# A decoder layer on one TensorE: q and k by Strassen's seven products, in a stage of their own ahead of the convolution's projections

## The chip, the cores and the metric

The kernel runs on one NeuronCore of a Trainium2 chip. The metric is the device time of one execution in microseconds. The kernel before takes 2086.06 us, the median of three runs (2084.89 to 2089.5).

## The reference

One decoder layer over 512 tokens of width 2048, all in float32. The combined input projection has columns q, k, v (1024 each: attention) and B, C, h (1024 each: a gated short convolution).

```
hn = rms_norm(x, norm_mix_pre)
q, k, v, gate_b, gate_c, hc = split(hn @ w_in)
a = diff_attention(q, k, v, lam, rel_bias)       # 8 heads of 128, two softmaxes of 64 each, causal
a = rms_norm(a, subln_gain) * (1 - lambda_init)
c = rms_norm(gate_b * short_conv(gate_c * hc, conv_w), conv_norm_gain)
x = x + rms_norm(concat(a, c) @ w_out, norm_mix_post)
hn = rms_norm(x, norm_ffn_pre)
f = (silu(hn @ w_gate) * (hn @ w_up)) @ w_down   # 5632 wide
x = x + rms_norm(f, norm_ffn_post)
```

The attention subtracts lam times a second softmax from the first; each head's scores get a bias by distance.

## The kernel before, in words

**Operands.** Every float32 operand of a product is held as two parts, high and low (`split`, L97 to L100: ScalarE casts the high part, VectorE subtracts it from the source for the low part). `mm3` (L121 to L130) makes one product of three matmuls: high by high (L124), high by low (L125), low by high (L126). Each matmul has its own weight load of 128 x 128.

**Places.** The transposed activations lie in `acts` as `act_hi` and `act_lo` (16 floats from the tile's start) and later, for the feed-forward part, as `ffn_hi` and `ffn_lo` (0 floats from the start). Behind `acts` in the same pool lie four ring slots of 2048 floats (`ring_tile`, L85), each a tile of its own. A weight chunk takes two slots (high, low); a Strassen operand of 128 columns takes one. A ring slot is written again when the products that read it are through. A pool that opens where another closed puts its tiles over the old ones, so a first write waits for the last read of the old tile.

**The order of the work.** A list of jobs (`add_job`, L157) is run in order by `run_jobs`. A job names the weight chunks that it needs; `run_jobs` loads them one chunk ahead (`load_chunk`: a 1 MB load on the queue of SyncE, then a split into two ring slots). A job is a generator: each time it yields, `side_step` lets every generator in the list `side` make one step. So what lies in `side` is placed between pieces of a job's matmuls. The tile framework places the instructions of each engine in an order of its own near the program's.

**Stages.** First the norm, the transposes of x and the first half of v's columns; then v's second half (`job_v`, 4 chunks of 4 yields, 12 matmuls of 512 columns each). Then, for each of four pairs of heads, `job_cols` (L342) for q, k, h, c and b: two halves of the contraction, each with two pieces of 24 matmuls (128 weights' columns by 512 tokens). `done_q` and `done_k` (L371 to L395) split q and k from PSUM. Behind k of a pair, the generator `heads` for its two heads goes into `side`: 12 steps beside the 12 pieces of h, c and b. A step does `scores` of one query tile, `values` of the tile two steps before, `weights` (the transposes of the softmax weights, L458) of the tile one step before, and sometimes `head_out`. v stays in SBUF (`v_sb`), as do `aT`, `cT` and the other tiles of the attention pool `attn`, opened right after the first stage. Then come the output projection (`job_out`), the feed-forward part by Strassen products (`ffn`: gate and up as 44 quartets of seven products with 24 matmuls of 256 columns; then down, 12 blocks of seven products in two halves) and the tail.

In gate and up, `prepare` makes the weights' operand of each product four products ahead: a sum or difference of two quarters of the weights (`combine`), then a split into one ring slot. `gather` adds the finished products. The moving operands are `acts` for four of the seven products and tiles named x for the sums of activations in the other three.

Of the kernel before, what the change touches and what calls it, by code (L numbers as in the profile page):

```python
# [18 lines left out]
P = 128  # L19
# [36 lines left out]
def trunk(ctx: ExitStack, tc: tile.TileContext, a, out):  # L56
# [45 lines left out]
    def rsqrt_mean(ss, n, width, eps, name):  # L102
# [3 lines left out]
        nc.gpsimd.tensor_tensor(out=r, in0=v, in1=mhalf[:, :n], op=ALU.pow)  # L106
        return r

    def load_chunk(src, n, m, name, parts=None):

        raw = wp.tile([P, n, m], F32, tag="raw", name=f"raw_{name}")
        nc.sync.dma_start(raw, src.rearrange("(n p) m -> p n m", p=P))
        if parts is None:
            hi = ring_tile(n, m, f"hi_{name}")
            lo = ring_tile(n, m, f"lo_{name}")
        else:
            hi, lo = parts(name)
        split(hi, lo, raw)
        return hi, lo

# [36 lines left out]
    def add_job(specs, go, ahead=1):  # L157
        jobs.append((specs, go, ahead))
# [25 lines left out]
    with start as sp:  # L184
# [124 lines left out]
    ap_ = at.enter_context(tc.tile_pool(name="attn", bufs=1))  # L309
    aT = ap_.tile([P, NH, S], F32, name="aT")  # L310
    cT = ap_.tile([P, 8, S], F32, name="cT")
    v_sb = ap_.tile([P, NT, A], F32, name="v_sb")
    sqacc = ap_.tile([P, S], F32, name="sqacc")

    klos = [ap_.tile([P, 2, S], F32R, name=f"klo{i}") for i in range(2)]
    for t in klos:
        nc.gpsimd.memset(t.bitcast(F32), 0.0)

    for t in range(NT):
        nc.scalar.copy(v_sb[:, t, :512], vb[t])  # L320

    def job_v(cg, q4, banks):
        def go(ch):
            (hi, lo), = ch
            for t in range(NT):
                if q4 == 0:
                    banks.append(mm_bank(f"pv_{cg}_{t}"))
                for k in range(4):
                    kc = 4 * q4 + k
                    mm3(banks[t], act_hi[:, t, kc, :], act_lo[:, t, kc, :], hi[:, k, :], lo[:, k, :], kc == 0, kc == KC - 1)  # L330
                if q4 == 3:
                    nc.scalar.copy(v_sb[:, t, cg * 512 : (cg + 1) * 512], banks[t])
                yield

        add_job([v_spec(cg, q4)], go)
# [4 lines left out]
    def job_cols(w, c0, name, done, after=None):  # L340

        banks = []  # L342

        def part(half):
            def go(ch):
                (hi, lo), = ch
                for j in range(2):
                    if half == 0:
                        banks.append(mm_bank(f"pc_{name}_{j}"))
                    for k in range(8):  # L350
                        kc = 8 * half + k
                        cs = slice(j * P, (j + 1) * P)
# [4 lines left out]
                if half == 1 and after is not None:  # L357
                    side.append(after())

            return go  # L360

        for half in range(2):
            add_job([col_spec(w, c0, half, name)], part(half))

    qk = {}

    halves = ((slice(0, QK), slice(QK, P)), (slice(QK, P), slice(0, QK)))  # L370

    def done_q(hp):
        def done(j, b):
            h = 2 * hp + j
            q = ap_.tile([P, 2, S], F32R, tag="q", bufs=2, name=f"q_{h}")
            for c, (own, other) in enumerate(halves):
                nc.scalar.copy(q[own, c, :], b[own, :])
                nc.vector.tensor_sub(q[other, c, :], b[own, :], q[own, c, :].bitcast(F32))
            qk["q", h] = q

        return done

    def done_k(hp):
        def done(j, b):
            h = 2 * hp + j
            k = ap_.tile([P, 2, S], F32R, tag="k", bufs=2, name=f"k_{h}")
            lo = klos[h % 2]
            for c, (own, other) in enumerate(halves):
                nc.scalar.copy(k[own, c, :], b[own, :])
                nc.scalar.copy(k[other, c, :], b[own, :])  # L390
                nc.vector.tensor_sub(lo[own, c, :], b[own, :], k[own, c, :].bitcast(F32))
            qk["k", h] = k, lo

        return done

    def heads(hs):

        at_ = [(h, qt) for h in hs for qt in range(NT)]
        st = {}
        for i in range(len(at_) + 4):  # L400
            if i < len(at_):
                scores(*at_[i], st)
            if 2 <= i <= len(at_) + 1:
                values(*at_[i - 2], st)
            if 1 <= i <= len(at_):
                weights(*at_[i - 1], st)
            if 4 <= i and at_[i - 4][1] == NT - 1:
                head_out(at_[i - 4][0], st)
            yield

    def scores(h, qt, st):
        if qt == 0:
# [10 lines left out]
        q, (k, klo), bt = qk["q", h], qk["k", h], st["bt", h]  # L423
        n = (qt + 1) * P
        qs = slice(qt * P, n)
        pss = [aux_bank(f"pss_{h}_{qt}_{c}") for c in range(2)]
# [347 lines left out]
    raws, heads_raw, operands, psq, tmp, slots, begun, made = {}, {}, {}, {}, {}, {}, {}, {}  # L774

    def slot(kind):

# [71 lines left out]
    def prepare(n):  # L849

        if n >= len(order):
            return prepare_down(n - len(order))
        q, i = order[n]
        if (q, i) in STAGED:

            if n < 2:
                w = wp.tile([P, 16, P], F32R, tag="raw", name=f"w_{q}_{i}")
            elif n == 2:
                w = place("spare", F32R, (P, 16, P))
            else:  # L860
                w = ring_tile(16, P, f"w_{q}_{i}")
            nc.sync.dma_start(w.rearrange("p k m -> p (k m)").bitcast(F32), stg[STAGED.index((q, i))])
            operands[n] = w.rearrange("p (a k) m -> p a k m", a=2)
        else:
            src = source(q, i)
            if i == 7 and q >= HEAD:
                combine(q, 3)
            if i == (3 if q == last_q else 6):
                combine(q, 2)
            if i == 3:  # L870
                combine(q, 4)
            w = ring_tile(16, P, f"w_{q}_{i}").rearrange("p (a k) m -> p a k m", a=2)
# [195 lines left out]
    def prepare_down(n):  # L1068
# [15 lines left out]
        w = ring_tile(2 * len(ks), 256, f"w_d{n}").rearrange("p (a k) m -> p a k m", a=2)  # L1084
        made["down"] = split(w[:, 0], w[:, 1], src)
        operands_d[n] = w
        if hf == 1:
# [125 lines left out]
    def tail_loads(i, hf):  # L1213
# [14 lines left out]
        if i == 4:  # L1228
            tail_split(1, tmp["tail", 1])
            for cg in (2, 3):  # L1230
                raw = tail_raw(cg, place(turns[count_b[0] % 3], F32, (P, 4, 512)))
                count_b[0] += 1
                ch[cg] = [ring_tile(4, 512, f"w_t{cg}_{part}") for part in range(2)]
                tail_split(cg, raw)

    def down_last(_):
# [69 lines left out]
```

## Time and profile before

| | |
|---|---|
| median of three runs | 2086.06 us |
| the profiled execution, its own time | 2091.33 us |
| its span, first to last instruction | 2089.5 us |
| TensorE busy | 2066.4 us (99%), 14604 matmuls |
| VectorE busy | 1499.9 us (72%) |
| ScalarE busy | 915.7 us (44%) |
| moved by DMA | 345.87 MB, 166 GB/s on the mean |
| granted TensorE clock | 0.996 |

PE is TensorE's matmuls, PEld its weight loads, DVE VectorE, ACT ScalarE, POOL GpSimd, SP the queue of SyncE that issues most DMAs. Tiles are named as in the program, out <- in. Matmuls are pipelined: a row's duration overlaps the next, so the pace is read from the starts. A `pc_q` is a bank of q's projection, `pv` of v's, `pss` scores, `ptw` transposed softmax weights, `pa` (from `w`, `acts`) and `pb` banks of gate and up, `pd` of down, `po` of the output projection. Where an instruction waited, the row's bracket or last column says how long and for whom.

### The profile page before, as it was taken

Reading aid. Unit: us, or ns where it says so; the run is one execution under the profiler, and the core shown is the slowest. Engines: PE = TensorE matmul, PEld = TensorE weight load, DVE = VectorE, ACT = ScalarE, POOL = GpSimd, SP = SyncE. Lnnn points to the kernel's source line nnn. Section 1 sums busy time; section 2 is a strip of 40 time slices with the busy share of each in tenths; the row PEclk is TensorE's granted clock in tenths of the full one; section 3 lists DMA queues with packets and bytes.
Section 4 is the critical chain, followed back from the end, with each engine's and each line's share of the span. In section 5 each row is a group of like instructions: output and inputs, shape, how many; then the busy total and the mean of one; then the engine's idle time right before and its main releaser. Section 6 shows DMA issues by size and latency. Waiting matters only on the chain.

```text
span 2089.5 us, 34251 instructions
## 1 busy us (share of the span) xinstructions
PE 2066.4 (99%) x14604; PEld 1927.1 (92%) x14604; DVE 1499.9 (72%) x1899; ACT 915.7 (44%) x1269; POOL 29.2 (1%) x51
## 2 busy tenths in 40 slices
PE   8999999999999999999999999999999999999998
PEld 6888888888888889999999999999999999999996
DVE  5226445363565368988888898988888777888887
ACT  4234343342444345444445544554544444444442
POOL 0000000000000000000000000000000000000000
PEclk9999999999999999999999999999999999999999
DMA  7432232223219868545454454454554965848454
GB/s 236 132 101 86 86 106 76 91 91 100 82 61 355 292 234 301 164 150 157 139 169 157 140 170 156 155 164 146 157 170 137 320 197 164 295 118 292 123 187 161
DMA packets 297049, 345.87 MB, mean 166 GB/s; under 512 B 11544, under 2 KB 261400, under 8 KB 291136
## 3 DMA queue, kind: packets, MB, share of 16 engines
q1 hardware_dynamic: 295296, 337.90, 49.5%
q10 hardware_dynamic: 1600, 5.79, 0.8%
q8 instruction: 114, 1.87, 0.4%
q14 instruction: 39, 0.32, 0.0%
HBM read 282.82 MB, written 63.46 MB: 166 GB/s over the span
## 4 chain that ended last, share of the span: by engine, by line
PE 93%; DVE 3%; DMA 2%; ACT 1%; issue 0%; SPq 0%; POOL 0%; POOLq 0%; DVEq 0%; ACTq 0%
PE pb L125 7%; PE pb L124 7%; PE pb L126 7%; PE pd L126 6%; PE pd L125 6%; PE pd L124 6%; PE pa L124 5%; PE pa L125 5%; PE pa L126 5%; PE po L124 3%; PE po L126 3%; PE po L125 3%; PE pv L125 1%; PE pv L126 1%; PE pv L124 1%; PE pc_h L124 1%
## 5 line engine op out<-in xcount | busy, mean ns | idle before, releaser
L125 PE MATMUL pb<-x,w 128*128 128x256 f32 x704 | 197.0, 280 | 0.0
L124 PE MATMUL pb<-x,w 128*128 128x256 f32 x704 | 196.6, 279 | 0.0
L126 PE MATMUL pb<-x,w 128*128 128x256 f32 x704 | 196.5, 279 | 0.0
L125 PE MATMUL pb<-acts,w 128*128 128x256 f32 x704 | 195.3, 277 | 0.0
L124 PE MATMUL pb<-acts,w 128*128 128x256 f32 x704 | 195.3, 277 | 0.0
L126 PE MATMUL pb<-acts,w 128*128 128x256 f32 x704 | 195.3, 277 | 0.0
L124 PE MATMUL pa<-acts,w 128*128 128x256 f32 x696 | 193.7, 278 | 0.0
L125 PE MATMUL pa<-acts,w 128*128 128x256 f32 x696 | 193.2, 278 | 0.0
L126 PE MATMUL pa<-acts,w 128*128 128x256 f32 x696 | 193.0, 277 | 0.0
L98 ACT CAST w<-raw_q 128x1024 fp32r<-128x1024 f32 x124 | 130.2, 1051 | 138.2 <-PE pb L126 66.1
L124 PE MATMUL pd<-w_d,acts 128*128 128x256 f32 x640 | 176.9, 276 | 1.0 <-DMA acts<-hx 1.0
L126 PE MATMUL pd<-w_d,acts 128*128 128x256 f32 x640 | 176.9, 276 | 1.0 <-DMA acts<-hx 1.0
L125 PE MATMUL pd<-w_d,acts 128*128 128x256 f32 x640 | 176.7, 276 | 0.0
L99 DVE TENSOR_TENSOR w<-raw_q,w 128x1024 fp32r<-128x1024 f32 x124 | 150.9, 1219 | 21.0 <-ACT w L98 20.7
L125 PE MATMUL pd<-w_d,x 128*128 128x256 f32 x480 | 132.6, 276 | 0.3 <-DVE w_d L99 0.3
L126 PEld LDWEIGHTS pb<-acts,w 128*128 128x128 f32 x704 | 132.8, 189 | 0.0
L124 PE MATMUL pd<-w_d,x 128*128 128x256 f32 x480 | 132.5, 276 | 0.0
L126 PE MATMUL pd<-w_d,x 128*128 128x256 f32 x480 | 132.5, 276 | 0.0
L124 PEld LDWEIGHTS pb<-x,w 128*128 128x128 f32 x704 | 132.3, 188 | 0.0
L125 PEld LDWEIGHTS pb<-acts,w 128*128 128x128 f32 x704 | 132.2, 188 | 0.0
L124 PEld LDWEIGHTS pb<-acts,w 128*128 128x128 f32 x704 | 132.2, 188 | 0.0
L125 PEld LDWEIGHTS pb<-x,w 128*128 128x128 f32 x704 | 132.1, 188 | 0.0
(304 smaller groups left out, 6074.5 us busy)
## 6 DMA issues: line engine op xcount, KB each, us to landing
raw_q<-in_w_gate SPq DMA_DIRECT2D x42, 1024.0 KB, 5.2
post<-in_w_up SPq DMA_DIRECT2D x22, 1024.0 KB, 5.2
pre<-in_w_up SPq DMA_DIRECT2D x22, 1024.0 KB, 5.4
hx<-spare SPq DMA_DIRECT2D x20, 896.0 KB, 8.5
hx<-m SPq DMA_DIRECT2D x20, 896.0 KB, 9.3
raw_o<-in_w_out SPq DMA_DIRECT2D x16, 1024.0 KB, 8.7
raw_b<-in_w_down SPq DMA_DIRECT2D x16, 896.0 KB, 6.3
acts<-hx SPq DMA_DIRECT2D x32, 448.0 KB, 9.0
```

Of the source, the lines that this page charges most:

```text
L98: first = nc.scalar.copy(hi, src)
L99: second = nc.vector.tensor_tensor(out=lo, in0=src, in1=hi.bitcast(F32), op=ALU.subtract)
L124: yield nc.tensor.matmul(o, lhsT=lhi, rhs=rhi, start=start, stop=False, **kw).ins
L125: yield nc.tensor.matmul(o, lhsT=lhi, rhs=rlo, start=False, stop=False, **kw).ins
L126: yield nc.tensor.matmul(o, lhsT=llo, rhs=rhi, start=False, stop=stop, **kw).ins
```

## The change

q and k are no longer projected between the convolution's columns. Right after v, a job `project` computes them in eight quartets (four pairs of heads, q and k) of Strassen's seven products, as gate and up do: tokens and the contraction are cut in halves, a weights' block of 256 columns in four quarters, and each product is 8 k x 3 matmuls of 256 columns. The four sums of activations (`t_sums`) are made beside v's second half into `t_all`. The tiles of this stage lie in a pool `wino`, opened where the attention pool was opened before and closed when the products are done; only then does the attention pool open. q, k and v are therefore written to DRAM (`qkd`, `vd`) and read again: v as a whole behind h's first job, q and k head by head into a part of `aT` that is not yet in use (`load_qk`, `prepare_head`, which splits them as `done_q` and `done_k` did). All eight heads are one generator of 37 steps, which starts beside c's first job. The raw weights and first operands of h are prepared inside `project`. `lamv` moves from the constants into `wino`. The ring becomes one tile of four slots 2080 floats apart in place of four tiles of 2048; the new stage uses each slot 16 floats further on, all others at its start.

```
-    ring = [0]
+    ring = [1]
+    ring_all = high.tile([P, 4 * (D + 32)], F32R, name="ring_all")
-    def ring_tile(n, m, name):
+    def ring_tile(n, m, shift=0):
         i = ring[0] = (ring[0] + 1) % 4
-        return high.tile([P, n, m], F32R, tag=f"ring{i}", name=name)
+        return ring_all[:, (D + 32) * i + shift :][:, : n * m].rearrange("p (n m) -> p n m", n=n)
...
+    wino = ExitStack()
+    wn = wino.enter_context(tc.tile_pool(name="wino", bufs=1))
+    t_all = wn.tile([P, 8 * D + 16], F32R, name="t_all")
+    odd_raw = [wn.tile([P, D], F32, name=f"odd{i}") for i in range(2)]
-    lamv = const.tile([P, 4, QK], F32, name="lamv")
+    lamv = wn.tile([P, 4, QK], F32, name="lamv")
...
+    def evacuate(cg, t, bank):
+        if t % 2 == 0:
+            tmp["v"] = wn.tile([P, 2, 512], F32, tag="r", bufs=2, name=f"r_v{cg}_{t}")
+        nc.scalar.copy(tmp["v"][:, t % 2, :], bank)
+        if t % 2:
+            nc.sync.dma_start(vd[:, t - 1 : t + 1, cg * 512 : (cg + 1) * 512], tmp["v"])
...
+    def open_attn(_):
+        wino.close()
+        ap_ = at.enter_context(tc.tile_pool(name="attn", bufs=1))
...
+    def load_attn(_):
+        load_qk(0)
+        nc.sync.dma_start(v_sb, vd)
+        side.append(heads(range(NH)))
...
                 if q4 == 3:
-                    nc.scalar.copy(v_sb[:, t, cg * 512 : (cg + 1) * 512], banks[t])
+                    evacuate(cg, t, banks[t])
+                    if t < 2:
+                        load_qk_raw(0, t)
+                    else:
+                        prepare_qk(t - 2)
...
+    def t_sums():
+        for tau in range(2):
+            a_, b_, c_, d_ = (odd_raw[j // 2][:, 1024 * (j % 2) :][:, :1024] for j in range(4))
...
+            whole(a_, 2 + tau, 0)
+            whole(b_, tau, 0)
+            nc.vector.tensor_sub(b_, a_, b_)
+            keep(5, b_)
+            yield
...
+    def prepare_qk(n):
...
+        if i in (7, 6, 3):
+            combine_qk(q, {7: 3, 6: 2, 3: 4}[i])
...
+        w = ring_tile(16, P, 16).rearrange("p (a k) m -> p a k m", a=2)
+        split(w[:, 0], w[:, 1], src)
...
+    def project(_):
+        for half in range(2):
+            load_qk_raw(1, half)
+        ready, st = 2, {}
+        for n, (q, i) in enumerate(order_qk):
...
+            for k in range(8):
+                mm3(o, w[:, 0, k, :], w[:, 1, k, :], xh[:, :, k, :], xl[:, :, k, :], k == 0 and i in (1, 5), k == 7, shared=True)
+            yield
...
+            while ready < n + 4:
+                prepare_qk(ready)
+                ready += 1
...
+    def load_qk(h):
+        if h < NH:
+            nc.sync.dma_start(aT[:, 6:8, :], qkd[:, h])
...
+    def prepare_head(h):
...
+        for c, (own, other) in enumerate(halves):
+            b = aT[own, 6, :]
+            nc.scalar.copy(q[own, c, :], b)
+            nc.vector.tensor_sub(q[other, c, :], b, q[own, c, :].bitcast(F32))
...
+        load_qk(h + 1)
...
     def heads(hs):
+        prepare_head(0)
+        yield
...
+            if i < len(at_) and at_[i][1] == 1 and at_[i][0] < NH - 1:
+                prepare_head(at_[i][0] + 1)
             yield
...
+    side.append(t_sums())
+    add_job([], project, ahead=0)
+    add_job([], open_attn, ahead=0)
     for p in range(4):
-        job_cols(w_in, p * 256, f"q{p}", done_q(p))
-        job_cols(w_in, A + p * 256, f"k{p}", done_k(p), after=lambda p=p: heads((2 * p, 2 * p + 1)))
         job_cols(w_in, 3 * A + 2 * A + p * 256, f"h{p}", done_h)
+        if p == 0:
+            add_job([], load_attn)
         job_cols(w_in, 3 * A + A + p * 256, f"c{p}", done_c(p))
         job_cols(w_in, 3 * A + p * 256, f"b{p}", done_b(p))
```

More of the change, by code (lines that the diff above doesn't have):

```diff
@@ L306, in trunk @@
             nc.sync.dma_start(cw[:, i, :], a["conv_w"][0, i].rearrange("(j p) -> p j", p=P))
-    at = ctx.enter_context(ExitStack())
[L309 to L320, printed above, removed]
+    vd = dram.tile([P, NT, A], F32, name="vd")
+    qkd = dram.tile([P, NH, 2, S], F32, name="qkd")
+    def evacuate(cg, t, bank):
[4 more added lines that the diff above has]
+            nc.sync.dma_start(vd[:, t - 1 : t + 1, cg * 512 : (cg + 1) * 512], tmp["v"])
+    tmp = {}
+    for t in range(NT):
+        evacuate(0, t, vb[t])
+    at = ctx.enter_context(ExitStack())
+    ap_ = aT = cT = v_sb = sqacc = klos = None
+    def open_attn(_):
+        nonlocal ap_, aT, cT, v_sb, sqacc, klos
+        wino.close()
+        ap_ = at.enter_context(tc.tile_pool(name="attn", bufs=1))
+        v_sb = ap_.tile([P, NT, A], F32, name="v_sb")
+        aT = ap_.tile([P, NH, S], F32, name="aT")
+        cT = ap_.tile([P, 8, S], F32, name="cT")
+        sqacc = ap_.tile([P, S], F32, name="sqacc")
+        klos = [ap_.tile([P, 2, S], F32R, name=f"klo{i}") for i in range(2)]
+        for t in klos:
+            nc.gpsimd.memset(t.bitcast(F32), 0.0)
+        return
+        yield
[3 more added lines that the diff above has]
+        side.append(heads(range(NH)))
+        return
+        yield
     def job_v(cg, q4, banks):
@@ L363, in job_cols, with t_part, whole, keep @@
             add_job([col_spec(w, c0, half, name)], part(half))
+    T_PLACE = {5: 0, 7: 1, 6: 2, 4: 3}
+    order_qk = [(q, i) for q in range(8) for i in (1, 5, 7, 2, 6, 3, 4)]
+    raws_qk, operands_qk = {}, {}
+    def t_part(i, part):
+        return t_all[:, 16 + (2 * T_PLACE[i] + part) * D :][:, :D].rearrange("p (t k n) -> p t k n", t=2, n=P)
+    def t_sums():
+        for tau in range(2):
+            a_, b_, c_, d_ = (odd_raw[j // 2][:, 1024 * (j % 2) :][:, :1024] for j in range(4))
+            def whole(o, t, half):
+                h_, l_ = (x_[:, t, 8 * half : 8 * half + 8, :].rearrange("p k n -> p (k n)").bitcast(F32) for x_ in (act_hi, act_lo))
+                nc.vector.tensor_add(o, h_, l_)
+            def keep(i, src):
+                split(*(t_part(i, part)[:, tau].rearrange("p k n -> p (k n)") for part in range(2)), src)
+            whole(a_, 2 + tau, 0)
[3 more added lines that the diff above has]
+            yield
+            whole(c_, 2 + tau, 1)
+            nc.vector.tensor_sub(a_, c_, a_)
+            keep(7, a_)
+            yield
+            nc.vector.tensor_sub(b_, c_, b_)
+            keep(6, b_)
+            yield
+            whole(d_, tau, 1)
+            nc.vector.tensor_sub(d_, d_, b_)
+            keep(4, d_)
+            yield
@@ new lines, in load_qk_raw @@
+    def load_qk_raw(q, half):
+        if half == 0:
+            if q % 2 == 0:
+                raws_qk[q] = [wp.tile([P, 8, 256], F32, tag="raw", name=f"raw_qk{q}_{i}") for i in range(2)]
+            else:
+                raws_qk[q] = [t.rearrange("p (k m) -> p k m", m=256) for t in odd_raw]
+        c0 = (q % 2) * A + (q // 2) * 256
+        nc.sync.dma_start(
+            raws_qk[q][half], w_in[half * 1024 : (half + 1) * 1024, c0 : c0 + 256].rearrange("(k p) m -> p k m", p=P)
+        )
@@ new lines, in combine_qk @@
+    def combine_qk(q, s):
+        (p11, p21), (p12, p22) = ((r[:, :, :P], r[:, :, P:]) for r in raws_qk[q])
+        if s == 1:
+            tmp["s1"] = wn.tile([P, 8, P], F32, tag="s1", name=f"s1_{q}")
+            nc.vector.tensor_add(tmp["s1"], p21, p22)
+        elif s == 3:
+            nc.vector.tensor_sub(p21, p11, p21)
+        elif s == 2:
+            nc.vector.tensor_sub(p21, p22, p21)
+        else:
+            nc.vector.tensor_sub(p12, p12, p21)
+    def prepare_qk(n):
+        if n >= len(order_qk):
+            return
+        q, i = order_qk[n]
+        if n == 0:
+            combine_qk(0, 1)
+        if i in (7, 6, 3):
+            combine_qk(q, {7: 3, 6: 2, 3: 4}[i])
+        (p11, p21), (p12, p22) = ((r[:, :, :P], r[:, :, P:]) for r in raws_qk[q])
+        src = {1: p11, 2: p12, 3: p12, 4: p22, 5: tmp["s1"], 6: p21, 7: p21}[i]
+        w = ring_tile(16, P, 16).rearrange("p (a k) m -> p a k m", a=2)
+        split(w[:, 0], w[:, 1], src)
+        operands_qk[n] = w
+        if i == 4 and q < 6:
+            for half in range(2):
+                load_qk_raw(q + 2, half)
@@ L365, in trunk @@
     qk = {}
+    def load_qk(h):
+        if h < NH:
+            nc.sync.dma_start(aT[:, 6:8, :], qkd[:, h])
     halves = ((slice(0, QK), slice(QK, P)), (slice(QK, P), slice(0, QK)))
[L372 to L394, printed above, removed]
+    def prepare_head(h):
+        q = ap_.tile([P, 2, S], F32R, tag="q", bufs=2, name=f"q_{h}")
+        k = ap_.tile([P, 2, S], F32R, tag="k", bufs=2, name=f"k_{h}")
+        lo = klos[h % 2]
+        for c, (own, other) in enumerate(halves):
+            b = aT[own, 6, :]
+            nc.scalar.copy(q[own, c, :], b)
+            nc.vector.tensor_sub(q[other, c, :], b, q[own, c, :].bitcast(F32))
+        for c, (own, other) in enumerate(halves):
+            b = aT[own, 7, :]
+            nc.scalar.copy(k[own, c, :], b)
+            nc.scalar.copy(k[other, c, :], b)
+            nc.vector.tensor_sub(lo[own, c, :], b, k[own, c, :].bitcast(F32))
+        qk[h] = q, k, lo
+        load_qk(h + 1)
@@ L773, in trunk @@
     order[-3:-1] = order[-2:-4:-1]
-    raws, heads_raw, operands, psq, tmp, slots, begun, made = {}, {}, {}, {}, {}, {}, {}, {}
+    raws, heads_raw, operands, psq, slots, begun, made = {}, {}, {}, {}, {}, {}, {}
     def slot(kind):
@@ L1232, in tail_loads @@
                 count_b[0] += 1
-                ch[cg] = [ring_tile(4, 512, f"w_t{cg}_{part}") for part in range(2)]
+                ch[cg] = [ring_tile(4, 512) for _ in range(2)]
                 tail_split(cg, raw)
```

71 lines of the change are left out of this document (58 added, 13 removed).

## The prediction

> **What bounds the kernel now.** I read the page first: busy shares, the 40 slices, the chain.
>
> ```profile
> PE 2066.4 (99%) x14604; PEld 1927.1 (92%) x14604; DVE 1499.9 (72%) x1899; ACT 915.7 (44%) x1269; POOL 29.2 (1%) x51
> PE   8999999999999999999999999999999999999998
> DVE  5226445363565368988888898988888777888887
> PEclk9999999999999999999999999999999999999999
> PE 93%; DVE 3%; DMA 2%; ACT 1%; issue 0%; SPq 0%; POOL 0%; POOLq 0%; DVEq 0%; ACTq 0%
> ```
>
> TensorE carries the chain at full clock, so fewer or faster matmuls are worth their own time unless a wait opens. But a modelled busy time can hide holes, so next came the windows of the stages that matter: second half of v, first q and k, twelve steps with attention, gate/up, down.
>
> ```profile
> 71.10:114.60 43.50, 43.48 (x192) 36.03 (x193) 8.17 (x5) 10.06 (x11) 1.92 (x6) 1.00 0.32 108
> 114.60:158.20 43.60, 43.60 (x194) 36.13 (x193) 13.30 (x10) 12.75 (x13) 0.00 (x0) 1.00 0.31 97
> 158.20:237.00 78.80, 78.80 (x391) 66.77 (x390) 45.88 (x112) 34.22 (x81) 4.18 (x5) 1.00 0.28 87
> 1050.00:1200.00 150.00, 150.00 (x1302) 150.00 (x1302) 130.86 (x140) 74.47 (x85) 0.00 (x0) 1.00 0.48 149
> 1700.00:1900.00 200.00, 199.71 (x1762) 199.51 (x1761) 161.01 (x176) 84.31 (x95) 0.00 (x0) 1.00 0.56 180
> ```
>
> After the length: PE busy (count), weight loads, DVE, ACT, POOL, clock, DMA share, GB/s. PE is full in each; DVE is at 31% beside q and k and 58% beside attention. The timeline gives the true pace, start to start:
>
> ```profile
> 114.77 0.39 PE L124 MATMUL pc_q<-acts,hi_q 128*128 128x512 f32 x1
> 136.53 0.39 PE L124 MATMUL pc_k<-acts,hi_k 128*128 128x512 f32 x1
> 158.29 0.39 PE L124 MATMUL pc_h<-acts,hi_h 128*128 128x512 f32 x1
> 603.17 0.48 PE L124 MATMUL po<-hi_o,acts 128*128 128x512 f32 x1
> ```
>
> The 96 matmuls of the first k take 158.29 − 136.53 = 21.76 us: 226.7 ns each, no hole. From q's first to the output projection's first are 488.4 us; the 1,920 matmuls of q, k, h, c and b (by the loops) fill 435.3, attention 53.1.
>
> **The change part by part: the products.** Removed: 8 projections x 96 = 768 matmuls 512 wide, 768 x 226.7 ns = 174.1 us. Added: 8 quartets x 7 products x 8 k x 3 = 1,344, 256 wide. Gate/up runs just this form (seven products, 168 matmuls a quartet), at two paces:
>
> ```profile
> 911.68 0.28 PE L126 MATMUL pb<-x,w 128*128 128x256 f32 x1
> 931.46 0.28 PE L126 MATMUL pb<-x,w 128*128 128x256 f32 x1
> 1034.58 0.39 PE L124 MATMUL pa<-acts,w 128*128 128x256 f32 x1
> 1050.43 0.28 PE L126 MATMUL pb<-x,w 128*128 128x256 f32 x1
> 1053.17 0.28 PE L126 MATMUL pa<-acts,w 128*128 128x256 f32 x1
> 1055.89 0.28 PE L126 MATMUL pb<-acts,w 128*128 128x256 f32 x1
> 1058.70 0.28 PE L126 MATMUL pb<-x,w 128*128 128x256 f32 x1
> 1069.81 0.28 PE L126 MATMUL pb<-x,w 128*128 128x256 f32 x1
> ```
>
> The first two rows are one quartet apart, the fourth and the last too: 19.78 us (117.7 ns) and 19.38 (115.4); the third row is where the pace turns. In the later quartet the 24 matmuls of an acts product take 2.72 us (113.3 ns) and of an x product 2.81 (about 117.5). I take 115.4, nearest as the same mix of tiles: 155.1 us. Bounds: 113.3 gives 152.3, 117.7 gives 158.2. **Term: −19.0 (−21.8 to −15.9).**
>
> **What feeds them.**
>
> ```profile
> L99 DVE TENSOR_TENSOR w<-raw_q,w 128x1024 fp32r<-128x1024 f32 x24 | 29.3, 1219 | 3.8 <-ACT w L98 3.8
> L834 DVE TENSOR_TENSOR m<-raw_q,raw_q 128x1024 f32<-128x1024 f32 x4 | 4.9, 1223 | 2.4 <-DMA raw_q<-in_w_gate 1.3 <-issue 1.1
> L948 DVE TENSOR_TENSOR m<-pa,m 128x256 f32<-128x256 f32 x7 | 3.0, 422 | 1.9 <-PE pa L126 1.9
> L959 DVE TENSOR_TENSOR m<-pb,m 128x512 f32<-128x512 f32 x8 | 5.5, 683 | 0.0
> L98 ACT CAST w<-raw_q 128x1024 fp32r<-128x1024 f32 x24 | 25.2, 1051 | 28.6 <-PE pb L126 12.9 <-DVE raw_q L840 9.2 <-issue 3.7
> L944 ACT COPY m<-pb 128x512 f32<-128x512 f32 x8 | 4.7, 584 | 4.9 <-PE pb L126 4.9
> L938 ACT COPY m<-pa 128x256 f32<-128x256 f32 x8 | 2.9, 365 | 6.5 <-PE pa L126 6.5
> ```
>
> A quartet asks DVE for 7 splits and 4 sums of about 1.22, three adds of 0.42 and one of 0.68: 15.4 us of 19.4; ACT for 7 x 1.05 + 0.58 + 2 x 0.37 = 8.7. Gate/up keeps PE full with DVE at 87% (130.86 of 150), so this costs nothing in steady state.
>
> **The entry.** The activation sums run beside the second half of v: per token pair 4 adds, 4 differences, 4 low splits, so 24 x 1.22 = 29.3 us of DVE on 8.17 now, in 43.5 us. They fit, but queue with the chunk splits.
>
> ```profile
> lamv<-in_lambda_q SPq DMA_DIRECT2D x2, 32.0 KB, 5.1
> L99 DVE TENSOR_TENSOR lo_h<-raw_h,hi_h 128x2048 fp32r<-128x2048 f32 x8 | 18.3, 2292 | 39.8 <-ACT hi_h L98 39.8
> raw_v<-in_w_in SPq DMA_DIRECT2D x8, 1024.0 KB, 5.6
> 71.12 0.50 PE L124 MATMUL pv<-hi_v,acts 128*128 128x512 f32 x1 [0.72 <-ACT v_sb L320]
> ```
>
> v's second half starts at 71.12. The sums with the third chunk's split end near 71.1 + 29.3 + 2.3 = 102.7, the fourth's low part at 105.0; its first use is 145 matmuls in, at 104.0: up to 1 us late. That split frees the buffer of q's second weight half: load 5.6, sum 1.22, splits, so about 113, and PE wants it at 114.8. If SP holds that load behind the store of v's second token tile (copied about 110), the weights come near 119: 4 us late. Also, `lamv` now lies over v's old tiles, so its loads (5.1 us) start near 71; were ACT's exponential of it queued ahead of the copies that free v's banks, PE would wait those 5 us at once. Nothing is to gain here but the 0.72 us ahead of this row. **Term: +3 (0 to +9).** v's new stores and reload are DMA beside 97 to 108 GB/s; the reload is issued a job (four steps, 22 us) before its use.
>
> **The exit.** h's first two chunks are split during the last three products and load_attn's three loads go out while h runs. Price 0; if a store held the pool's release, `hs`, first written 72 matmuls or 16 us into h, would be late, not PE's operands.
>
> **Attention packed closer.** PE's 53.1 us of attention stay. 37 steps must fit into the 44 that follow h0 (c0 to b3). A step is then 24 x 226.7 ns + 53.1 / 37, 6.9 us. Now twelve steps hold two heads, then three.
>
> ```profile
> L98 ACT CAST hi_h<-raw_h 128x2048 fp32r<-128x2048 f32 x8 | 15.2, 1906 | 30.1 <-PE pc_k L125 21.3 <-issue 8.9
> L378 DVE TENSOR_TENSOR q<-pc_q,q 64x512 fp32r<-64x512 f32 x16 | 11.0, 689 | 13.4 <-ACT q L377 13.2
> L390 ACT CAST k<-pc_k 64x512 fp32r<-64x512 f32 x16 | 9.3, 582 | 0.2
> L509 DVE SCALAR_TENSOR_TENSOR cT<-hs,cw,cT 128x512 f32<-128x512 f32 x16 | 11.9, 743 | 0.0
> L519 DVE TENSOR_TENSOR cT<-pc_b,cT 128x512 f32<-128x512 f32 x7 | 4.8, 686 | 10.8 <-PE pc_b L126 10.8
> 217.82 0.75 DVE L447 SCALAR_TENSOR_TENSOR e<-e,rs 128x512 f32<-128x512 f32 x1
> 218.84 0.60 PE L458 MATMUL ptw<-ident,e 128*128 128x128 f32 x4
> ```
>
> Of DVE's 45.88 us in twelve steps, six chunk splits are 13.8 and the convolution about 8 (estimate: twelve operations of 128x512 between these two rows), so a head is 12. Three heads with four 0.69 us splits of q and k each make 36 + 8.3 + 21.8 = 66 of 83 us, 80%. ACT: 34.22 − 11.4 − 2.4 leaves 10.2 a head; 30.6 + 18 x 0.58 + 13.8 = 55, 66%. Capacity is there; slack is not everywhere: the widest tile's weights end at 218.57 and PE transposes them at 218.84, 0.27 us later. The chunk's split now falls on the other parity of steps, away from the widest tile, and the new 2.8 us on the second tile of a head. I expect a handful of stalls of a few tenths. **Term: +2 (0 to +16, 0.5 us in each of 32 steps).**
>
> On SP, the load of the next head's q and k waits until ACT and DVE have read this head's; behind it stand bt and the next chunk. A chunk needs 5.6 + 1.9 + 2.3 = 9.8 us, a job is two steps, 13.8, and SP is let go two steps before: hidden.
>
> **The ring.** The change also moves three of the four ring slots by 128, 256 and 384 bytes for the rest of the kernel. Whether an address sets the pace shows in the rows above: equal instructions, 113.3 on acts, 117.5 on x; but acts at unchanged addresses went from the longer to the shorter pace at 1034, so it is not the address alone. The loops count 7,392 matmuls in gate/up and 3,360 in down; at the longer pace are 44 x 72 on x and about 12 x 96 on acts, 4,320; down is at the shorter (200 us / 1,762). If one slot in four has the longer pace everywhere, 2,688 are there: −1,630 x 4.4 ns = −7. Bounds: all 6,432 matmuls that are now at 113.3 to 113.5 ns fall to 117.7, +28; all others rise, −19. I take half, since the history counted too. **Term: −4 (−19 to +28).**
>
> The page "TensorE: Matmul & The Clock Gate" of the Trainium skill (Part 2, "Step-by-step: what each phase is for") says that TensorE has two independent SBUF read ports, so loading the next weights takes nothing from the running matmul. By it the slots' addresses cost nothing and the sum is −14; the two paces of equal instructions show that it does not explain everything here, though no row shows the cause.
>
> **Sum.** −19 + 3 + 2 − 4 = −18. The profiled execution took 2091.3 us (span 2089.5) and would take 2073; the median of the three runs, 2086.1, becomes 2068.
>
> **The rivals.** *Slots count for nothing:* 2072. For it, the change of pace at fixed addresses. 0.22.
>
> *Late entry:* both weight halves and the fourth chunk late by full loads, and stores holding the new pool: 9 at the entry and one 5.6 us load more before h, 15 in place of the 3: 2080. Against it, SP has two steps of freedom. 0.10.
>
> *Attention becomes the bound:* the 0.27 us slack turns negative in each of 32 steps by 0.5 us on average, 16 us: 2082; it decides from 0.5 us a step on. Against it, 80% of DVE. 0.08.
>
> *Slower, the ring slows the feed-forward part:* the moved slots meet the moving rows, and of 6,432 fast matmuls three quarters fall to 117.7 ns: +21, in place of −4, so 2093. It makes the kernel slower from some 4,100 such matmuls on (4.4 ns each eat 14 us and 0.2%). For it: both paces exist. Against it: down keeps 113.5 over two kinds of tile. 0.08.
>
> *The change doesn't shorten the products:* weight loads, 150.00 us busy in 150 in gate/up, pace the 256-wide form at above 129.5 ns (174.1 / 1,344); the time stays at about 2087. Against: 115 to 118 ns where they are full already. 0.02.
>
> **How the numbers follow.** The forecast has 0.50, own range 2058 to 2079. The range starts where the products run at 113.3 ns, nothing stalls and the slots bring 12: 2052; it reaches past the late entry and the late attention to 2085 and leaves out the slow ring, the unshortened products and tails. About 0.2%, 4 us, is what can be told from no change here. Faster (below 2082): forecast and neutral slots nearly whole, over half of the late entry, a third of the late attention, 0.79. Same 0.11, slower 0.10.
>
> **What would show it.** Right: 168 matmuls of a q/k quartet in about 19.4 us, the stage near 155; first q product within 3 us of v's end; holes of PE beside c, b and h below 3 us in sum; gate/up quartets between 19.1 and 19.8. Wrong: products above 20 us, PE waiting for ptw or pss in most steps, or down above 115 ns.

## The result, and the profile after

The changed kernel took 2096.85 us in the median of five runs (2095.52 to 2099.54), the kernel before 2087.68 in five (2084.89 to 2089.5): a ratio of 1.0047 [1.0033, 1.0062]. The change made the kernel slower by about 9 us, where 18 less were forecast. The profiled execution took 2097.92 us, 6.6 more than that of before.

First the page of after, the same lines as for before:

```profile
PE 2072.3 (99%) x15180; PEld 1957.8 (93%) x15180; DVE 1609.6 (77%) x2027; ACT 958.8 (46%) x1341; POOL 25.3 (1%) x51
PE   8999999999999999999999999999999999999998
DVE  5777747777455478988888889888888777878887
PEclk9999999999999999999999999999999999999999
PE 92%; DVE 4%; DMA 2%; issue 1%; ACT 1%; SPq 0%; POOL 0%; DVEq 0%; POOLq 0%; ACTq 0%
```

TensorE still carries the chain, at the same clock, with no slice emptier than before. It has 576 more matmuls, as the loops say (1,344 − 768). Nothing on this page tells why they take longer than planned. The windows by stage do; their columns are those of the prediction's (after the length PE, PEld, DVE, ACT, POOL with counts, clock, DMA share, GB/s):

```profile
71.10:115.60 44.50, 44.28 (x192) 36.01 (x193) 38.38 (x38) 18.06 (x21) 0.00 (x0) 1.00 0.46 157
115.60:272.20 156.60, 156.60 (x1345) 156.56 (x1344) 114.60 (x115) 68.81 (x81) 0.00 (x0) 1.00 0.38 124
650.00:710.00 60.00, 60.00 (x264) 49.15 (x263) 24.29 (x17) 18.70 (x20) 0.00 (x0) 1.00 0.91 316
1050.00:1200.00 150.00, 150.00 (x1290) 150.00 (x1290) 131.84 (x141) 74.41 (x85) 0.00 (x0) 1.00 0.51 159
1700.00:1900.00 200.00, 199.79 (x1699) 199.59 (x1698) 156.29 (x168) 81.32 (x92) 0.00 (x0) 1.00 0.55 179
```

Read the last two rows against the prediction's rows for the same windows. PE is as full as it was, at a clock of 1.00, and yet gate/up starts 1,290 matmuls in 150 us in place of 1,302, and down 1,699 in 200 us in place of 1,762: in down 117.7 ns each in place of 113.5. Busy time cannot show this, for a matmul that starts later behind the one ahead of it counts as just as busy. Only the count in a window, or the starts, show it. The third row is the output projection, 264 in 60 us; before had two more:

```profile
650.00:710.00 60.00, 60.00 (x266) 49.70 (x265) 31.64 (x24) 23.26 (x24) 0.00 (x0) 1.00 0.97 334
```

The timeline of after gives the ends of the new stages: first product of q and k, first of h, first of the output projection, first of gate/up.

```profile
115.80 0.28 PE L133 MATMUL pqk_a<-acts,ring_all 128*128 128x256 f32 x1
272.37 0.39 PE L133 MATMUL pc_h<-acts,ring_all 128*128 128x512 f32 x1
590.76 0.39 PE L133 MATMUL po<-ring_all,acts 128*128 128x512 f32 x1
775.24 0.28 PE L133 MATMUL pa<-acts,w 128*128 128x256 f32 x1
```

From the first of q to the first of the output projection are 474.96 us; they were 488.4. So the part that was rewritten became 13.4 us shorter, and the output projection begins 12.4 us earlier. Everything behind it, whose code is the same, gives that back and more. And these are all the waits of PE above 0.6 us (line, engine waited for, us in total, times, longest):

```profile
PE pv L133 <- ACT acts L99: 2.8, 1, 2.8
PE pt_pre L146 <- DVE xn L156: 2.3, 1, 2.3
PE pd L133 <- DMA ring_all<-stg: 2.2, 1, 2.2
PE pa L133 <- ACT m L1119: 2.0, 1, 2.0
PE warm L266 <- POOL mhalf L96: 1.5, 1, 1.5
PE pv L134 <- DVE ring_all L100: 1.3, 1, 1.3
PE px L836 <- DVE m L156: 1.1, 2, 0.7
PE pv L133 <- ACT r_v L331: 0.7, 1, 0.7
```

No wait for scores, for transposes or for q's weights is among them. The lost time is not waiting; it is pace.

The stages of all the runs that follow, in us, from one profiled execution each, start to start of the stages' first matmuls (down runs to some 443 matmuls before the last, which with the end make the tail of 79.8 to 81.3). "Places" is where the four ring slots lie modulo 512 bytes, relative to one another. q and k stand ahead of the convolution's stage in the kernels with the change (156.6 in after, 158.3 in all others).

| kernel | places of the slots | conv + attention | out | gate/up | down | median |
|---|---|---|---|---|---|---|
| before | equal | (q to b 488.4) | 182.7 | 865.9 | 357.8 | 2087.7 |
| after | 128 B apart | 318.4 | 184.5 | 871.3 | 368.5 | 2096.9 |
| after_even | equal | 314.7 | 182.6 | 864.1 | 355.6 | 2073.1 |
| before_moved | 128 B apart | (q to b 498.9) | 184.1 | 867.0 | 370.5 | 2117.8 |
| after_all32 | equal, all 128 B on | 319.5 | 186.1 | 877.3 | 355.9 | 2094.8 |
| after_half | 256 B apart | 314.7 | 182.6 | 861.4 | 355.7 | 2072.3 |
| after_even_pad | equal, other tiles 384 B on | 314.2 | 182.8 | 860.2 | 358.6 | 2061.8 |
| after_even_pad64 | equal, other tiles 256 B on | 314.7 | 182.6 | 863.5 | 358.2 | 2073.7 |
| pad_stops | as after_even_pad | 314.2 | 182.8 | 880.0 | 367.8 | 2101.5 (one run) |
| before_pad | equal, other tiles 384 B on | (q to b 488.5) | 182.9 | 852.4 | 358.5 | 2083.4 |

### The profile page after: what moved, and what is told of

It reads as the page before. It is cut to its first block, busy times and chain, and to the rows that moved or that the text cites. A ratio compares the mean times of both kernels' runs of the same rounds, so it can differ in the third digit from the quotient of the medians.

```text
span 2096.1 us, 35907 instructions
## 1 busy us (share of the span) xinstructions
PE 2072.3 (99%) x15180; PEld 1957.8 (93%) x15180; DVE 1609.6 (77%) x2027; ACT 958.8 (46%) x1341; POOL 25.3 (1%) x51
## 4 chain that ended last, share of the span: by engine, by line
PE 92%; DVE 4%; DMA 2%; issue 1%; ACT 1%; SPq 0%; POOL 0%; DVEq 0%; POOLq 0%; ACTq 0%
PE pb L134 7%; PE pb L133 7%; PE pb L135 7%; PE pd L133 6%; PE pd L134 6%; PE pd L135 6%; PE pa L133 5%; PE pa L134 5%; PE pa L135 5%; PE po L134 3%; PE po L133 3%; PE po L135 3%; PE pv L134 1%; PE pv L135 1%; PE pv L133 1%; PE pc_h L135 1%
## 5 line engine op out<-in xcount | busy, mean ns | idle before, releaser
L99 ACT CAST ring_all<-raw_q 128x1024 fp32r<-128x1024 f32 x124 | 130.0, 1050 | 195.2 <-PE pb L134 79.6
L134 PE MATMUL pb<-x,ring_all 128*128 128x256 f32 x704 | 197.2, 280 | 0.0
L135 PE MATMUL pb<-x,ring_all 128*128 128x256 f32 x704 | 197.0, 280 | 0.0
L133 PE MATMUL pb<-x,ring_all 128*128 128x256 f32 x704 | 196.9, 280 | 0.0
L135 PE MATMUL pb<-acts,ring_all 128*128 128x256 f32 x704 | 195.5, 278 | 0.4 <-DVE ring_all L100 0.4
L133 PE MATMUL pb<-acts,ring_all 128*128 128x256 f32 x704 | 195.7, 278 | 0.0
L134 PE MATMUL pb<-acts,ring_all 128*128 128x256 f32 x704 | 195.5, 278 | 0.0
L133 PE MATMUL pa<-acts,ring_all 128*128 128x256 f32 x680 | 190.8, 281 | 2.0 <-ACT m L1119 2.0
L134 PE MATMUL pa<-acts,ring_all 128*128 128x256 f32 x680 | 189.9, 279 | 0.0
L135 PE MATMUL pa<-acts,ring_all 128*128 128x256 f32 x680 | 189.8, 279 | 0.0
L135 PE MATMUL pd<-ring_all,acts 128*128 128x256 f32 x640 | 179.1, 280 | 0.6 <-DMA acts<-hx 0.6
L133 PE MATMUL pd<-ring_all,acts 128*128 128x256 f32 x640 | 179.2, 280 | 0.0
L134 PE MATMUL pd<-ring_all,acts 128*128 128x256 f32 x640 | 179.2, 280 | 0.0
L100 DVE TENSOR_TENSOR ring_all<-raw_q,ring_all 128x1024 fp32r<-128x1024 f32 x124 | 151.2, 1220 | 27.2 <-ACT ring_all L99 26.9
L100 DVE TENSOR_TENSOR ring_all<-pre,ring_all 128x1024 fp32r<-128x1024 f32 (+1 forms) x106 | 122.0, 1153 | 54.4 <-ACT ring_all L99 53.5
L100 DVE TENSOR_TENSOR ring_all<-post,ring_all 128x1024 fp32r<-128x1024 f32 (+1 forms) x106 | 121.7, 1148 | 21.7 <-ACT ring_all L99 21.4
L134 PE MATMUL pd<-ring_all,x 128*128 128x256 f32 x480 | 134.6, 280 | 0.2 <-DVE ring_all L100 0.2
L135 PE MATMUL pd<-ring_all,x 128*128 128x256 f32 x480 | 134.4, 280 | 0.0
L133 PE MATMUL pd<-ring_all,x 128*128 128x256 f32 x480 | 134.4, 280 | 0.0
L133 PEld LDWEIGHTS pb<-x,ring_all 128*128 128x128 f32 x704 | 133.3, 189 | 0.0
```

Of the source, the lines that this page charges most:

```text
L99: first = nc.scalar.copy(hi, src)
L100: second = nc.vector.tensor_tensor(out=lo, in0=src, in1=hi.bitcast(F32), op=ALU.subtract)
L133: yield nc.tensor.matmul(o, lhsT=lhi, rhs=rhi, start=start, stop=False, **kw).ins
L134: yield nc.tensor.matmul(o, lhsT=lhi, rhs=rlo, start=False, stop=False, **kw).ins
L135: yield nc.tensor.matmul(o, lhsT=llo, rhs=rhi, start=False, stop=stop, **kw).ins
```

## The experiments

The theory: the slots' new places slow the matmuls, everywhere, and the rest of the change does what it was forecast to do. The rival: the place counts for nothing, and what slows the later stages is something else that the change brought, such as one tile for the whole ring (tracked and waited for as one), more DMA, or another order of the buffers. The kernel before took 2087.15 us beside the first four kernels and 2088.43 beside the last four (medians of 17 runs each); ratios are against these.

**after_even: the change with the slots at equal places.** The ring stays one tile; its slots lie 2048 floats apart again, as the four tiles did before, and the pool keeps its size modulo 512 bytes, so that all other tiles stay where they were.

```
-    ring_all = high.tile([P, 4 * (D + 32)], F32R, name="ring_all")
+    ring_all = high.tile([P, 4 * D + 128], F32R, name="ring_all")
...
-        return ring_all[:, (D + 32) * i + shift :][:, : n * m].rearrange("p (n m) -> p n m", n=n)
+        return ring_all[:, D * i + shift :][:, : n * m].rearrange("p (n m) -> p n m", n=n)
```

> The changed kernel with its ring slots 2048 floats apart again, all at the same place within 512 bytes, as before the change; the new stage still uses each slot 16 floats on. Ring theory (the moved slots slow the weight loads or the moving reads in every stage behind): the output projection back from 184.5 to about 182.7 us, gate and up from 871.3 to 866 or less, down from 368.5 to 357.8, in all about 20 us less than the changed kernel, near 2076. Rival, history (the new stage or the packed attention leaves TensorE or the memories in another state, whatever the addresses): down stays at 368, total 2090 to 2097. Rival, one tile in place of four: stays at 2097 too.

Measured: 2073.13 us (2070.33 to 2075.07), against before 0.9931 [0.9919, 0.9943]: 23.7 us less than after by one number in an address. Its windows, as above:

```profile
650.00:710.00 60.00, 60.00 (x266) 49.69 (x265) 20.95 (x15) 18.47 (x20) 0.00 (x0) 1.00 0.93 334
1050.00:1200.00 150.00, 150.00 (x1302) 150.00 (x1302) 132.72 (x140) 75.48 (x86) 0.00 (x0) 1.00 0.50 155
1700.00:1900.00 200.00, 199.71 (x1762) 199.51 (x1761) 162.57 (x178) 83.72 (x94) 0.00 (x0) 1.00 0.60 203
```

The counts of before are back to the matmul: 266, 1,302, 1,762. And its stages:

```profile
114.88 0.28 PE L133 MATMUL pqk_a<-acts,ring_all 128*128 128x256 f32 x1
273.18 0.39 PE L133 MATMUL pc_h<-acts,ring_all 128*128 128x512 f32 x1
587.86 0.39 PE L133 MATMUL po<-ring_all,acts 128*128 128x512 f32 x1
770.46 0.28 PE L133 MATMUL pa<-acts,w 128*128 128x256 f32 x1
```

The convolution with all of the attention takes 587.86 − 273.18 = 314.68 us. Only the places differ between this kernel and after, so the places are shown to cause the loss, and one tile, DMA and order are cleared. What in the hardware makes them count is not shown by this.

**before_moved: the kernel before with only the slots moved.** To make room, the block that computes lambda's factor from `lamv` stands behind the attention pool's tiles, and `lamv` in that pool.

```
+    ring_all = high.tile([P, 4 * (D + 32)], F32R, name="ring_all")
...
-        return high.tile([P, n, m], F32R, tag=f"ring{i}", name=name)
+        return ring_all[:, (D + 32) * i :][:, : n * m].rearrange("p (n m) -> p n m", n=n)
...
-    lamv = const.tile([P, 4, QK], F32, name="lamv")
+    lamv = ap_.tile([P, 4, QK], F32, name="lamv")
```

> The kernel before with only the ring changed: one tile, slots 2080 floats apart (lamv moved into the attention pool to make room, nothing else). Ring theory: gate and up plus down lose about 16 us, the 512-wide stages some 5 more, near 2108. History rival: unchanged, 2087, since q and k and the attention are where they were. One-tile rival: slower too, so this run and the first together tell it from the ring's places.

Measured: 2117.77 us (2115.37 to 2118.64), 1.0144 [1.0129, 1.0159]. The windows of the first q and k, of the output projection, gate/up and down:

```profile
114.60:158.20 43.60, 43.60 (x188) 35.12 (x187) 13.30 (x10) 12.74 (x13) 0.00 (x0) 1.00 0.30 97
650.00:710.00 60.00, 60.00 (x264) 49.17 (x263) 35.77 (x29) 28.00 (x35) 0.00 (x0) 1.00 0.98 336
1050.00:1200.00 150.00, 150.00 (x1289) 150.00 (x1288) 130.53 (x137) 74.94 (x86) 0.00 (x0) 1.00 0.50 155
1700.00:1900.00 200.00, 199.80 (x1703) 199.59 (x1702) 155.83 (x166) 82.05 (x93) 0.00 (x0) 1.00 0.54 175
```

The same loss without Strassen: 188 matmuls where before had 194, 1,703 where it had 1,762. It is the larger for the 1,920 matmuls of q, k, h, c and b, 512 wide, which take 10.5 us more, twice what was expected. One thing besides the number of these matmuls differs: the ring begins one slot earlier here (`ring = [0]`, in after `[1]`), so that a chunk's high part lies in the slots at 128 and 384 bytes, where after has the low part; the matmuls of h take 233.3 ns on the mean here and 231.1 in after (from the starts). Gate/up lost only 1.1 us, but not because its matmuls were spared: counting what start-to-start distances above 130 ns have beyond 118, PE's waits there are 4.2 us in place of before's 6.9. Without them gate/up takes 862.9, like after's 862.7, against 859.1 in before. As after_even shows that one tile alone costs nothing, the cost is that of the slots and belongs to no other part of the change.

**after_all32: all four slots moved by 128 bytes alike.** This tells a difference between the slots from their distance to the tiles of the matmul's other operand. For h, c, b, gate and up the slots hold what is loaded as weights, and `acts` or x streams; in the output projection and down the slots hold what streams, and `acts` or x is loaded.

```
-    ring_all = high.tile([P, 4 * (D + 32)], F32R, name="ring_all")
+    ring_all = high.tile([P, 4 * D + 128], F32R, name="ring_all")
...
-        return ring_all[:, (D + 32) * i + shift :][:, : n * m].rearrange("p (n m) -> p n m", n=n)
+        return ring_all[:, D * i + 32 + shift :][:, : n * m].rearrange("p (n m) -> p n m", n=n)
```

> The changed kernel with the slots 2048 floats apart, all moved by 32 floats (128 bytes). If the place of a slot against the moving rows sets the pace (ring theory, by pairs): the output projection is slow for all chunks, 512-wide matmuls at 232 to 234 ns in place of 227 (188 us in place of 183), and so are h, c and b; gate and up may gain, since slot and x tiles then stand 64 bytes apart as slot and acts did before. If only the mixing of four places matters: every stage as in the run with equal places at 0. History rival: as the changed kernel.

Measured: 2094.79 us (2083.93 to 2097.39, three of ten runs near 2084 and seven near 2095), 1.0026 [1.001, 1.0042].

```profile
650.00:710.00 60.00, 60.00 (x260) 48.66 (x259) 24.08 (x18) 20.70 (x21) 0.00 (x0) 1.00 0.93 321
1050.00:1200.00 150.00, 150.00 (x1276) 150.00 (x1276) 128.84 (x138) 73.44 (x84) 0.00 (x0) 1.00 0.49 154
1700.00:1900.00 200.00, 199.71 (x1762) 199.51 (x1761) 161.65 (x176) 84.84 (x96) 0.00 (x0) 1.00 0.55 179
```

Both halves count, and differently by width. The 512-wide matmuls are at their slowest (260; out and conv the longest of the table): for them it is the distance to the other operand's tile, whether the slots are loaded or stream. Down is back at 1,762: there, in this kernel, it is enough that the slots are alike. Gate/up, where a gain was thought possible, lost the shorter pace in nearly all its products (150 / 1,276 = 117.6 ns). The profiled execution is one of the seven; what the three did otherwise is not known.

**after_half: slots 256 bytes apart.** The rival was that any inequality costs.

```
-    ring_all = high.tile([P, 4 * (D + 32)], F32R, name="ring_all")
+    ring_all = high.tile([P, 4 * D + 256], F32R, name="ring_all")
...
-        return ring_all[:, (D + 32) * i + shift :][:, : n * m].rearrange("p (n m) -> p n m", n=n)
+        return ring_all[:, (D + 64) * i + shift :][:, : n * m].rearrange("p (n m) -> p n m", n=n)
```

> The changed kernel with slots 2112 floats apart: two places in turn, 256 bytes apart. If a distance of 256 bytes counts as none (512-wide matmuls ran at 226.5 ns at 0 and 256 and at 230 to 234 at 128 and 384): the output projection back at about 182.7 us and h, c and b at 314. If the 256-wide matmuls of gate, up and down suffer from any change of place from product to product: down stays near 368, total near 2088. If only distances of 128 bytes hurt them: down at 356, total near 2074.

Measured: 2072.30 us (2069.19 to 2074.6), 0.9933 [0.9918, 0.9949].

```profile
650.00:710.00 60.00, 60.00 (x266) 49.69 (x266) 20.95 (x15) 18.45 (x20) 0.00 (x0) 1.00 0.91 331
1050.00:1200.00 150.00, 150.00 (x1303) 150.00 (x1302) 131.26 (x140) 75.62 (x86) 0.00 (x0) 1.00 0.52 160
1700.00:1900.00 200.00, 199.71 (x1762) 199.51 (x1762) 162.56 (x178) 83.51 (x94) 0.00 (x0) 1.00 0.62 207
```

Nothing is lost: 256 bytes count as no distance. Of the places tried for the slots only odd multiples of 128 bytes cost. After has both kinds side by side: by the order of the slots, its output projection streams a chunk's high part from the slots at 0 and 256 bytes and the low part from those at 128 and 384. From the fourth chunk on the matmuls on high parts took 226.2 ns and those on low parts 234.3 (from the starts).

**after_even_pad: after_even with the x tiles moved.** In before, from 1034 us on, the acts products have the shorter pace and the x products the longer. A tile of 96 floats that nothing uses, ahead of `ident`, moves the tiles of its side by 384 bytes, so that x stands to the slots as acts does.

```
+    const.tile([P, 96], F32, name="pad")
     ident = const.tile([P, P], F32, name="ident")
```

> Equal places, and all left tiles moved by 384 bytes, so that the x tiles stand to the slots as acts do. By pairs: the x products of gate and up go from 117.7 to 113.3 ns, 44 x 72 x 4.4 ns = 14 us less than the run with equal places, about 2062. If the slow pace of x comes from something else (another tile, a place in memory): no change against that run.

Measured: 2061.84 us in the median of six, 0.9893 [0.9868, 0.9919], the fastest kernel here, faster than before and after. But the six spread over 20 us: 2071.55, 2060.27, 2061.45, 2076.68, 2056.89, 2062.22. The profiled one, 2071.55, shows why. Windows between PE's short waits:

```profile
925.00:1460.00 535.00, 534.98 (x4718) 534.59 (x4717) 471.14 (x502) 269.58 (x307) 0.00 (x0) 1.00 0.52 159
1462.00:1618.00 156.00, 156.00 (x1327) 156.00 (x1326) 133.00 (x141) 77.86 (x89) 0.00 (x0) 1.00 0.52 161
```

```profile
1461.23 0.38 PE L134 MATMUL pa<-acts,ring_all 128*128 128x256 f32 x1 [0.23 <-ACT m L1120]
```

For 535 us every product, acts and x, ran at 113.4 ns. Then PE stood for a moment, and the same loop went on at 117.6 ns. No address changed there. The pace is also a state that lasts while PE runs on. The turn at 1034 us in before, which the prediction put down to history, stands behind such a moment too:

```profile
1034.58 0.19 PEld L124 LDWEIGHTS pa<-acts,w 128*128 128x128 f32 x1 [0.20 <-ACT m L938]
```

There PE waited 0.20 us; the acts products had taken 117.7 ns up to it and took 113.3 to 113.5 from it on, while the x products stayed at 117.8.

**after_even_pad64: the pad with 64 floats.** It moves the tiles by 256 bytes, which the slots did not feel.

```
+    const.tile([P, 64], F32, name="pad")
```

> Equal places, left tiles moved by 256 bytes in place of 384: x tiles stand 192 bytes before the slots, acts 64, the two distances that down ran well with. By pairs of places: gate and up near 837 us (113.3 ns throughout), total near 2060 in every run. If a pace once lost stays lost until the next stop of TensorE, whatever the pair: runs between 2057 and 2077, as with 384 bytes.

Measured: 2073.73 us (2068.72 to 2075.44), 0.9934 [0.9921, 0.9946].

```profile
1050.00:1200.00 150.00, 150.00 (x1303) 150.00 (x1302) 131.98 (x140) 75.78 (x86) 0.00 (x0) 1.00 0.50 155
```

This is after_even again, acts at 113 to 114 ns and x at 117.8. So the distance from the slots to x is not all; 256 bytes count as none here too, and the 384 of the other pad did something that these do not.

**pad_stops: after_even_pad with PE stopped at quartets of gate/up.** If the pace is drawn when PE starts again after a stop, more stops give more changes, and only there. A VectorE operation adds zero times the last element of the previous quartet's bank to one element of the next weights (no value changes); PE must wait for it.

```
         for n, (q, i) in enumerate(order):
+            if i == 1 and q > HEAD and q not in CLOSE and q - 1 not in CLOSE:
+                o, w = psq[q - 1]["b"], operands[n]
+                nc.vector.scalar_tensor_tensor(
+                    out=w[:, 0, 0, 0:1], in0=o[:, 511:512], scalar=0.0, in1=w[:, 0, 0, 0:1].bitcast(F32), op0=ALU.mult, op1=ALU.add
+                )
             product(n)
```

> Equal places with 384 bytes of pad, and a tiny operation of VectorE between the quartets of gate and up, on the end of one quartet's last product and ahead of the next one's first weights, so that TensorE stops for half a microsecond to two at each quartet. If a stop draws the pace anew (lock theory): quartets of 113.3 and of 117.7 ns side by side, changing at the stops only. If places alone set the pace: all quartets alike. The whole time says nothing, since some 36 stops are added.

Measured, in one run: 2101.46 us. The waits, and windows of 18.8 us, each inside one quartet between two stops:

```profile
PE pa L134 <- DVE ring_all L1345: 14.3, 29, 1.1
```

```profile
1113.60:1132.40 18.80, 18.80 (x166) 18.80 (x167) 14.38 (x15) 8.88 (x11) 0.00 (x0) 1.00 0.35 113
1133.10:1151.90 18.80, 18.80 (x160) 18.80 (x161) 17.67 (x20) 8.90 (x10) 0.00 (x0) 1.00 0.59 182
1153.50:1172.30 18.80, 18.80 (x166) 18.80 (x167) 14.38 (x15) 8.89 (x11) 0.00 (x0) 1.00 0.35 114
1173.00:1191.80 18.80, 18.80 (x160) 18.80 (x161) 17.68 (x20) 8.91 (x10) 0.00 (x0) 1.00 0.59 180
1371.40:1390.20 18.80, 18.80 (x166) 18.80 (x167) 17.70 (x20) 9.44 (x11) 0.00 (x0) 1.00 0.61 185
1531.50:1550.30 18.80, 18.80 (x166) 18.80 (x167) 17.55 (x20) 9.39 (x11) 0.00 (x0) 1.00 0.61 185
```

A quartet has 166 matmuls in its window (113.3 ns) or 160 (117.5), and keeps its pace from one stop to the next, as do all others of gate/up with a stop on either side. The first four rows alone would let DMA or VectorE be the cause, for the slower quartets have the heavier traffic (0.59 against 0.35). The last two rows have that traffic and more, and the shorter pace. So in this kernel the pace is settled at the stop. What settles it is not shown. Of the 30 us above after_even_pad's profiled run, 14.3 are the idle time at the stops, and gate/up takes 5.5 more for its slower quartets and the starts behind stops; down, in which nothing was added, drew the longer pace from 1730 to its end and lost 9.2.

**before_pad: the pad alone on the kernel before.**

```
+    const.tile([P, 96], F32, name="pad")
     ident = const.tile([P, P], F32, name="ident")
```

> The kernel before with the left tiles moved by 384 bytes and nothing else. If the places of the x tiles bound gate and up before, too: up to 14 us less than before, near 2073, or between that and before from run to run. If not: 2087.

Measured: median 2083.38 us of ten, nine of them between 2073.35 and 2088.36 and one of 9128.41 that nothing here explains; 0.9969 [0.9952, 0.9986].

```profile
1050.00:1200.00 150.00, 150.00 (x1326) 150.00 (x1325) 133.25 (x142) 76.40 (x87) 0.00 (x0) 1.00 0.49 152
```

In this execution all products of this window had the shorter pace (150 / 1,326 = 113.1 ns), and gate/up took 852.4 us in place of 865.9. So the pad's effect isn't the change's, and it is there in some executions more than in others.

## Why the prediction was wrong

**The failed step is the ring.** The prediction put it at −4, from "If one slot in four has the longer pace everywhere, 2,688 are there: −1,630 x 4.4 ns = −7". That step took the pace for a property of each slot by itself, some gaining and some losing, and it only counted the 256-wide matmuls. The runs show +23.7 (after against after_even, medians). By stages, in the profiled runs: v +0.8, q and k −1.7, convolution +3.7, output projection +1.9, gate/up +7.2, down +12.9, the tail +1.1, together 25.9 between two executions 25.95 apart. Slots at unlike places took the shorter pace from nearly every matmul of down, not from one slot's in four (117.7 ns on the mean, from the starts), and they took time from 512-wide matmuls, which the term left out: 227.7 to 231.2 ns for c (after_even and after).

The rival "the ring slows the feed-forward part" had this mechanism and nearly its price, +21 (gate/up, down and the tail lost 21.2), with a chance of 0.08. What was held against it, that down kept 113.5 ns over two kinds of tile, was weak evidence: both kinds met four slots that lay alike, so nothing in the trace of before had tried unlike ones. The bounds from rows, −19 to +28, held the +23.7; the middle value with a minus sign had no row behind it, and the range left the upper bound out.

**The other terms held.** Without the ring they made −19 + 3 + 2 = −14, and after_even, the change with the slots as they were, took 2073.13 against 2087.15: −14.0. Singly:

- *Products, −19.0.* 156.6 us in after for 155.1 forecast (116.5 ns each), 158.3 in after_even (117.8 ns, the upper bound of 158.2): −17.5 and −15.8. The middle value rested on a mix of paces by tile, which did not come: in after_even the products on `acts` and on the sums in `t_all` all ran at 117.7 to 117.8 ns. In after those on `t_all` ran at 115.4 to 116.0, so this one stage gained by the unlike slots. VectorE, 114.60 of 156.60 us, did not hold them.
- *Entry, +3.* About 0. v's second half took 44.5 us, 0.8 above before's 43.6, and in after_even 43.7: the 0.8 is the slots' pace. There is no hole ahead of the first product, and the wait ahead of v's second half is 0.7 as it was. The upper bound, made from a load queued behind a store, was not needed.
- *Exit, 0.* h's first matmul follows the last product without a wait.
- *Attention packed closer, +2.* 0.4: 314.7 us in after_even, where 1,152 matmuls at 226.7 ns and the 53.1 of attention make 314.3. PE waited for no transpose and no score; the slack of 0.27 us in before did not turn into a wait.

So the hit of −14.0 is partly luck: the terms as measured in after_even make −15.8 + 0 + 0.4 = −15.4. Its profiled execution is 19.4 below that of before (2071.97 and 2091.33); the other 4.0 lie in gate/up (1.8) and down (2.2), within what the pace changes from run to run, and aren't counted to the change.

**The rule of the read ports.** The page "TensorE: Matmul & The Clock Gate" of the Trainium skill (Part 2, "Step-by-step: what each phase is for") states that two independent SBUF read ports keep weight loads from taking read bandwidth from a running matmul. The prediction's reading of it, that the slots' addresses then cost nothing, is not what the traces show: equal matmuls of down take 113.5 or 117.7 ns by where the ring's slots lie (after_even and after). Whether the ports are what is shared was not measured. The sum by that reading, −14, is what the kernel does when the slots lie alike.

Of the marks named for wrong, "down above 115 ns" came true, and of those for right, the stage near 155, the first product right behind v, and no holes beside c, b and h; gate/up quartets, 19.1 to 19.8 forecast, came to 19.8 (871.3 / 44).

## What to carry to other kernels

When tiles are merged or a pool is laid out anew, compare where the operands of the matmuls lie modulo 256 bytes, and keep the slots of a ring alike: here 128 bytes between them cost 24 us of 2,073, more than the 15.8 that the new products brought. Judge TensorE's pace by the number of matmuls that start in a window, not by its busy time, which is full at either pace. And where a term's bounds are −19 and +28 and no row tries the new arrangement, the sign is not known: make the loss a case of its own with a real chance, or keep the addresses.

## What the runs showed of the hardware

- A stream of equal matmuls has two paces at full clock: 113.3 and 117.7 ns at 256 columns; at 512 columns about 226.7 and 230 to 234 (the mean over q to b in before and the slots of the output projection in after, from the starts).
- At 512 columns the pace goes with the distance between the weights' and the moving rows' addresses. Modulo 512 bytes: alike or 256 apart 226 to 227; 64, 128, 384 or 448 apart 230 to 234 (from the programs' addresses and the starts). At 256 columns that is not the rule: in the kernels without the 96-float pad it was enough for down that the four slots were alike modulo 256 bytes (after_all32: 113.3 to 113.7 ns at distances of 64 and 448). With that pad down had the longer pace too, for a while or from 1730 us to its end (after_even_pad, pad_stops), and the products of q and k ran at 117.7 to 117.8 ns with like slots.
- At 256 columns the pace is a state as well: with the 96-float pad it ran through acts and x products alike until PE stopped, and was chosen anew at a stop (pad_stops; after_even_pad at 1461). Times of that kernel spread over 20 us for it, where after_even spread over 5.

What stays open: what in TensorE or its reads makes the two paces, what chooses one at a stop, and why the 384-byte pad lets x products take the shorter one while 256 bytes don't. That the reads of the weights and of the moving rows get in each other's way would fit the distances, but that is only argued; no run measured a read by itself.
